# A decoder trunk on one Trainium2 core: turn-back sums of the state-space loop on TensorE, gate weights split after the loop, and another dealing-out of the table work

## The chip, the cores and the metric

The kernel runs on one core of one Trainium2 chip. The metric is the device time of one execution in microseconds. Times given as "the median" are over three timed runs; one further execution was taken by the hardware profiler, and all rows below are from that one.

## The reference, cut to what matters

Two layers of a trunk, on x of shape (1, 512, 1024) in float32. Each layer is FFN, token mixer, FFN, each between RMSNorms; the mixer of the first layer is the S5 state-space layer, that of the second a convolution module. The change touches the first FFN and the S5 layer:

```python
def swiglu(h, w1, w3, w2):
    return (jax.nn.silu(h @ w1) * (h @ w3)) @ w2

# s5_mixer: 64 groups, each with 64 complex states over 512 positions
u = (h @ w_in).reshape(bsz, seq, 64, 16)
... abar (decay and turn of each state), bb (its input weights) from dt, a, b
bu_re, bu_im = einsum(u, bb_re), einsum(u, bb_im)
_, _, st_re, st_im = lax.associative_scan(_complex_scan_op, elems, axis=1)
y = einsum(st_re, c_re) - einsum(st_im, c_im) + d_skip * u
y = gelu(y)
z = y * sigmoid(y @ w_glu + b_glu)
return z @ w_out
```

## The kernel before, in words

**Products.** Features lie on the 128 partitions, the 512 positions along the free axis. A weight unit is 128x1024 float32 (0.5 MB), that is eight 128x128 blocks. Each dense product is made of three fp32r products (`mm3`, lines 110 to 112): high weight part by high input part, high by low, low by high. `want(n)` makes the two parts of all units up to n: SP loads the raw unit (line 83, three raw buffers), ScalarE casts the high part (line 94), VectorE subtracts to get the low part (line 98). The load of unit u+3 is issued behind the split of unit u and waits for its raw buffer. Every engine works through its own queue in program order.

**First FFN.** 44 units of the up product (`ffn`), then 22 units of the down product (`proj`), 24 products each. Beside it the tables of the S5 layer are computed: generators, of which `tick(queue, budget)` runs some steps in every unit, until the estimated costs of the steps (in us) have used up the budget; what is overspent is taken off the next tick. The queue "D" (parameters, rotation tables) is served in the up product with the budget `PREP_UP`, the queue "P" in the down product with `PREP_DOWN`: first `s5_ops` for six tiles (costs 2.5 and 0.85 a tile), then `s5_in` for eight tiles (two steps of 2.1 a tile, lines 695 to 697 and 702 to 704, whose operands `bt` and `fb` come by the DMAs of lines 684 and 687). What is left of a queue is run by `flush` ahead of the last output block.

**S5 loop.** Eight tiles of 128x512, each four blocks of 128 (blocks of positions and features are regrouped through DRAM). The states are turned by a rotation, so that the recurrence is a real decay, scanned, and turned back. Step s issues `inputs(s)` (TensorE, line 867, 8 float32 products of 128 columns), `back(s-1)` (line 895 on), table loads for later tiles, and then, by the letters of `S5_ORDER[s]`: `stack` (k, line 855), `turn` (t, lines 880 to 885), `want` (w), `parts` (p, high and low part of y of tile s-3, lines 940 and 941), `state` (s, line 909), `decay` (d), `outputs(s-1)` (o, TensorE, lines 918 to 920, 12 float32 products), `scan` (c, line 892, two scans), `glu_step` (g, 12 fp32r products of the gate product) and `gelu` (l). The string `S5_ENG` says which engine does which sum or product:

```python
eng[0].tensor_tensor(X[:, 0], X[:, 0], Y[:, 0], op=A)        # turn, 882, POOL
eng[1].tensor_tensor(X[:, 1], X[:, 1], Y[:, 1], op=D)        # turn, 885, POOL
eng[2].tensor_tensor(S[:, 1, :, 1:], Y[:, 0, :, :n], s, op=M)  # back, 901, POOL
eng[3]... 902 DVE; eng[4]... 903 DVE; eng[5]... 904 POOL
eng[6].tensor_tensor(S[:, 1, :, 1:], S[:, 1, :, 1:], Y[:, 1, :, :n], op=A)  # 905, POOL
eng[7].tensor_tensor(st[i][:, 0, :, 1:], X[:, 0, :, :n], X[:, 1, :, :n], op=D)  # state, 909, DVE
```

`S5_WANT` says up to which unit step s splits: all eight gate units (u0+8 to u0+15) are split inside the loop. Only the first four of the eight output blocks of the gate product (`g4`) are accumulated in the loop; the other four (`h4`) come after it, and their products cover the trip of the last y through DRAM. Then follow `gates` for both halves and the output product.

Of the kernel before, what the change touches and what calls it, by code (L numbers as in the profile page):

```python
# [7 lines left out]
F32 = mybir.dt.float32  # L8
# [13 lines left out]

C_TAPS = (31, 31, None, None, None, None, None, 23)
NL = 2
S5_ORDER = ("sktwdopcgl", "sktwdopcgl", "stwdopcgkl", "skwtdopcgl", "skwtdopcgl", "skwtdolpcg", "skwtdopcgl", "skwtdopcgl", "skwtdopcgl")
S5_ENG = "PPPDDPPD"
S5_WANT = (8, 9, 10, 11, 11, 13, 14, 14, 15)
BUD_D = (3, 8, 18, 18, 18, 18)
FFN_AHEAD = 4

PREP_UP, PREP_DOWN = 2.8, 3.4
S5_FIRST = 2


# [1 line left out]
def trunk(ctx: ExitStack, tc: tile.TileContext, h, plan):  # L36
# [15 lines left out]
    def page(dt=F32R):  # L52
        return pages.tile([P, 2, T], dt, tag="pg", name=nm("pg"))
# [352 lines left out]
    def ffn(e, post, pre, defer=True):  # L406
        u0, xn = e["u"], e["xn"]
        g = []

        def evac(m, pa, pb):  # L410
            a = tmp()
            DVE.tensor_tensor(a, pa, e["y"], op=ALU.mult)  # L412
            ACT.activation(a, a, AF.Silu)  # L413
            DVE.tensor_tensor(a, pb, a, op=ALU.mult)  # L414
            t = page()
            ACT.copy(t[:, 0, :], a)  # L416
            DVE.tensor_tensor(t[:, 1, :], a, t[:, 0, :].bitcast(F32), op=ALU.subtract)  # L417
            g.append(t)

        pend = None  # L420
        want(u0 + 6)
        for m in range(2, NF):
            pa, pb = psum(), psum()
            for j, ps in enumerate((pa, pb)):
                want(u0 + 2 * m + j)
                for k in range(NK):
                    mm3(ps, u0 + 2 * m + j, k, xn[k][:, 0, :], xn[k][:, 1, :], k == 0, k == NK - 1)
                    if m == 2 and j == 0 and k == 4:
                        entry_norm(e, True)
                    if k == 3:  # L430
                        tick("D", PREP_UP)
            if FFN_AHEAD and m > 2:
                want(u0 + 2 * m + FFN_AHEAD)
            if m == 2:
                ACT.preload_act_table(AF.Silu)
                evac(0, e["ps"][0], e["ps"][1])
                evac(1, e["ps"][2], e["ps"][3])
            else:
                evac(*pend)
            pend = m, pa, pb  # L440
            want(u0 + 2 * m + 2)
        evac(*pend)
        return proj(u0 + 2 * NF, NF, g, post, 1, pre, g[:NK], carried=e["acc"], defer=defer)
# [234 lines left out]
    def s5_in():  # L678

        M, A, S = ALU.mult, ALU.add, ALU.subtract  # L680

        def load(i):
            bt, fb = page(F32), page(F32)
            nc.sync.dma_start(out=flat(bt), in_=h["s5b"][i, :, :1024])
            for t in range(4):
                src = f_d[t * 64 + i * 8 : t * 64 + i * 8 + 8, :].rearrange("r c -> (r c)")
                nc.sync.dma_start(out=flat(fb)[32 * t : 32 * t + 32, :], in_=src.partition_broadcast(32))
            return bt, fb

        nxt = load(0)  # L690
        yield
        for i in range(8):
            bt, fb = nxt
            t = page(F32)
            DVE.tensor_tensor(t[:, 0, :], fb[:, 1, :], bt[:, 1, :], op=M)
            DVE.tensor_tensor(t[:, 1, :], fb[:, 1, :], bt[:, 0, :], op=M)
            DVE.tensor_tensor(fb[:, 1, :], fb[:, 0, :], bt[:, 1, :], op=M)
            cost[0] += 2.1
            if i < 7:
                nxt = load(i + 1)  # L700
            yield
            DVE.tensor_tensor(fb[:, 0, :], fb[:, 0, :], bt[:, 0, :], op=M)
            DVE.tensor_tensor(fb[:, 0, :], fb[:, 0, :], t[:, 0, :], op=S)
            DVE.tensor_tensor(fb[:, 1, :], fb[:, 1, :], t[:, 1, :], op=A)
            nc.sync.dma_start(out=tab_d[i, :, 0:1024], in_=flat(fb))
            cost[0] += 2.1
            yield
# [124 lines left out]
    def s5(e, post, pre):  # L832
        u0, xn = e["u"], e["xn"]
        M, A, D = ALU.mult, ALU.add, ALU.subtract
        tabs, wk, st, yf, yhl, ys = {}, {}, {}, {}, {}, {}
        eng = [POOL if c == "P" else DVE for c in S5_ENG]
        quad = lambda v: v.rearrange("p (q c) -> p q c", q=4)
        n = P - 1

# [36 lines left out]
        def turn(i):  # L876
            b0, b1 = wk[i]
            c, s = tabs[i][2][:, 0], tabs[i][2][:, 1]
            X, Y = (page(F32).rearrange("p r (q c) -> p r q c", q=4) for _ in range(2))
            DVE.tensor_tensor(X[:, 0], b0, c, op=M)  # L880
            DVE.tensor_tensor(Y[:, 0], b1, s, op=M)
            eng[0].tensor_tensor(X[:, 0], X[:, 0], Y[:, 0], op=A)
            DVE.tensor_tensor(X[:, 1], b1, c, op=M)
            DVE.tensor_tensor(Y[:, 1], b0, s, op=M)
            eng[1].tensor_tensor(X[:, 1], X[:, 1], Y[:, 1], op=D)
            wk[i] = X, Y

        def scan(i):
# [5 lines left out]
                )  # L894

        def back(i):
            X, Y = wk[i]
            c, s = (tabs[i][2][:, r, :, :n] for r in range(2))
            S = st[i] = page(F32).rearrange("p r (q c) -> p r q c", q=4)
            POOL.memset(S[:, :, :, 0:1], 0.0)  # L900
            eng[2].tensor_tensor(S[:, 1, :, 1:], Y[:, 0, :, :n], s, op=M)
            eng[3].tensor_tensor(X[:, 1, :, :n], Y[:, 1, :, :n], s, op=M)  # L902
            eng[4].tensor_tensor(Y[:, 1, :, :n], Y[:, 1, :, :n], c, op=M)  # L903
            eng[5].tensor_tensor(X[:, 0, :, :n], Y[:, 0, :, :n], c, op=M)
            eng[6].tensor_tensor(S[:, 1, :, 1:], S[:, 1, :, 1:], Y[:, 1, :, :n], op=A)

        def state(i):
            X, Y = wk.pop(i)
            eng[7].tensor_tensor(st[i][:, 0, :, 1:], X[:, 0, :, :n], X[:, 1, :, :n], op=D)

        def outputs(i):
            q, mu = tabs[i][1], tabs[i][3]
            del tabs[i]
            S = st.pop(i)
            ps = psum()
            for j in range(4):
                o = ps[:, j * P : j * P + P]
                PE.matmul(o, lhsT=mu[:, 0, j, :], rhs=mu[:, 1, j, :], start=True, stop=False)
                PE.matmul(o, lhsT=q[:, 0, j, :], rhs=S[:, 0, j, :], start=False, stop=False)
                PE.matmul(o, lhsT=q[:, 1, j, :], rhs=S[:, 1, j, :], start=False, stop=True)  # L920
            return ps

        def gelu(i, ps):
# [13 lines left out]
        def parts(i):  # L937
            if i >= 0:
                t = yhl[i] = page()
                ACT.copy(t[:, 0, :], yf[i])  # L940
                DVE.tensor_tensor(t[:, 1, :], yf[i], t[:, 0, :].bitcast(F32), op=D)
# [14 lines left out]
        def glu_step(j0, bank, k):  # L956
            if k >= 0:
                for j in range(4):
                    mm3(bank[j], g0 + j0 + j, k, yhl[k][:, 0, :], yhl[k][:, 1, :], k == 0, k == NK - 1)

        load(0, (0, 3, 2))
        load(1, (0, 3, 2))
# [14 lines left out]
        for s in range(9):  # L977
            if s <= 7:
                inputs(s)
            if s <= 1:  # L980
                win(6 + s)
            if s == 3:
                g4.extend(psum() for _ in range(4))
            if s:
                back(s - 1)

            y_out(s - 2)
            load(s + 2, (0,))
            unstack(s + 2)
            load(s + 2, (2,))  # L990
            load(s + 1, (1,))
            y_in(s - 2)
            load(s + 3, (3,))
            wu = u0 + S5_WANT[s]
            for c in S5_ORDER[s]:
                if c == "t" and s <= 7:
                    turn(s)
                if c == "p":
                    parts(s - 3)
                if c == "s" and s:  # L1000
                    state(s - 1)
                if c == "k":
                    stack(s + 3)
                if c == "w":
                    want(wu)
                if c == "d":
                    decay(s + 1)
                if c == "c" and s <= 7:
                    scan(s)
                if c == "g":  # L1010
                    glu_step(0, g4, s - 3)
                if c == "o" and s:
                    po = outputs(s - 1)
                if c == "l" and s:
                    gelu(s - 1, po)
# [14 lines left out]

        y_out(7)
        parts(6)
        want(g0 + 7)
        y_in(7)
        h4.extend(psum() for _ in range(4))
        for k in range(3):
            glu_step(4, h4, k)
        glu_step(0, g4, 6)
        parts(7)
        glu_step(0, g4, 7)  # L1040
        ACT.preload_act_table(AF.Sigmoid)
        gates(g4, 0)
        for k in range(3, 8):
            glu_step(4, h4, k)
        want(g0 + 11)
        gates(h4, 4)
        return proj(
# [436 lines left out]
```

## Time and profile before

| | us |
|---|---|
| median of 3 runs | 1935.65 (1930.0 to 1937.69) |
| profiled execution | 1930.56 |
| its span, first to last instruction | 1928.4 |
| TensorE busy | 1867.4 (97%) |
| VectorE busy | 1100.8 (57%) |
| ScalarE busy | 636.9 (33%) |
| GpSimd (POOL) busy | 89.2 (5%) |

TensorE's mean granted clock is 0.988 of full speed. The first FFN lies at about 0 to 400 us of the span, the S5 layer at about 420 to 620 us, its loop at 438 to 538 us. A busy share is an average over the whole span; stretches are read one by one.

### The profile page before, as it was taken

To read this page: it belongs to the slowest core of one execution; us is meant where nothing else is said; L and a number is where in the kernel's file an instruction comes from. 1 tells how busy PE (TensorE), PEld (TensorE's weight loads), DVE (VectorE), ACT (ScalarE), POOL (GpSimd) and SP (SyncE) were. 2 spreads that over 40 slices of the span, in tenths; PEclk is the share of its full clock that TensorE was granted. 3 is DMA by queue.
4 is the path that set the end of the run, shared out by engine and by line. 5 is a ranking of instruction groups with operands and counts; after the bars stand their busy time and mean duration, and the time that the engine had idled before them with its cause. 6 is when DMAs were issued, how large, how long until landed. Compare 5 with 4: busy or idle time off the path is not lost.

```text
span 1928.4 us, 23797 instructions
## 1 busy us (share of the span) xinstructions
PE 1867.4 (97%) x9374; PEld 1587.3 (82%) x9374; DVE 1100.8 (57%) x1886; ACT 636.9 (33%) x920; POOL 89.2 (5%) x79
## 2 busy tenths in 40 slices
PE   9999999897799999999999999999999999999997
PEld 7788888796678888888898888888898888888886
DVE  6887465688946743432285433334995785343324
ACT  4323454251233532322244222223422653222211
POOL 2000000006700000000000000000000000000000
PEclk9999999998899999999999999999999999999998
DMA  4345458738522332222224322223464124232231
GB/s 159 110 134 156 136 134 252 238 141 303 184 83 77 106 113 98 89 86 98 88 77 131 101 96 88 76 99 98 170 230 142 52 70 153 88 101 85 89 98 44
DMA packets 101279, 235.04 MB, mean 122 GB/s; under 512 B 26160, under 2 KB 44080, under 8 KB 101168
## 3 DMA queue, kind: packets, MB, share of 16 engines
q1 hardware_dynamic: 99872, 232.46, 37.0%
q8 instruction: 73, 1.20, 0.3%
q10 hardware_dynamic: 1296, 1.07, 0.2%
q14 instruction: 38, 0.31, 0.1%
HBM read 209.77 MB, written 23.72 MB: 121 GB/s over the span
## 4 chain that ended last, share of the span: by engine, by line
PE 86%; DVE 9%; DMA 2%; issue 1%; ACT 1%; SPq 1%; POOLq 0%; POOL 0%; DVEq 0%; ACTq 0%
PE ps L112 27%; PE ps L111 27%; PE ps L110 27%; PE ps L1199 2%; DMA pg<-f_d 1%; DVE pg L98 1%; DVE pg L892 1%; PE ps L1166 1%; DVE x L354 1%; DVE tmp L350 1%; PE ps L740 1%; DVE pg L902 1%; PE ps L117 0%; DVE pg L186 0%; DVE pg L903 0%
## 5 line engine op out<-in xcount | busy, mean ns | idle before, releaser
L110 PE MATMUL ps<-pg,pg 128*128 128x512 f32 (+1 forms) x2808 | 1036.8, 369 | 7.4 <-ACT pg L1333 4.7
L112 PE MATMUL ps<-pg,pg 128*128 128x512 f32 (+1 forms) x2808 | 1029.8, 367 | 9.9 <-DVE pg L98 9.8
L111 PE MATMUL ps<-pg,pg 128*128 128x512 f32 (+1 forms) x2808 | 1031.8, 367 | 4.8 <-DVE pg L186 3.3
L112 PEld LDWEIGHTS ps<-pg,pg 128*128 128x128 f32 x2808 | 531.5, 189 | 97.9 <-DVE pg L98 11.9
L111 PEld LDWEIGHTS ps<-pg,pg 128*128 128x128 f32 x2808 | 531.6, 189 | 96.6 <-DVE pg L186 7.9
L110 PEld LDWEIGHTS ps<-pg,pg 128*128 128x128 f32 x2808 | 532.3, 190 | 95.5 <-ACT pg L1333 5.1
L98 DVE TENSOR_TENSOR pg<-raw,pg 128x1024 fp32r<-128x1024 f32 x305 | 368.3, 1244 | 109.9 <-ACT pg L94 63.5
L94 ACT CAST pg<-raw 128x1024 fp32r<-128x1024 f32 x310 | 311.2, 1047 | 108.7 <-DMA raw<-w 43.5
L414 DVE TENSOR_TENSOR tmp<-ps,tmp 128x512 f32<-128x512 f32 x88 | 60.9, 692 | 248.3 <-PE ps L112 219.2
L276 DVE TENSOR_TENSOR acc<-acc,tmp 128x512 f32<-128x512 f32 (+1 forms) x54 | 33.0, 611 | 255.2 <-ACT tmp L271 255.1
L413 ACT ACTIVATE tmp<-tmp 128x512 f32<-128x512 f32 x88 | 55.6, 632 | 284.8 <-DVE tmp L412 284.8
L416 ACT CAST pg<-tmp 128x512 fp32r<-128x512 f32 x88 | 54.6, 621 | 252.1 <-DVE tmp L414 249.5
L271 ACT ACTIVATE tmp<-ps 128x512 f32<-128x512 f32 (+1 forms) x45 | 24.3, 540 | 293.4 <-PE ps L112 293.0
L417 DVE TENSOR_TENSOR pg<-tmp,pg 128x512 fp32r<-128x512 f32 x88 | 61.0, 693 | 61.8 <-ACT pg L416 61.8
L412 DVE TENSOR_TENSOR tmp<-ps,y 128x512 f32<-128x512 f32 x88 | 60.4, 686 | 27.4 <-PE ps L112 27.4
L173 ACT ACTIVATE pg<-x,gsc 128x256 fp32r<-128x256 f32 x80 | 40.8, 510 | 67.8 <-DVE x L354 67.8
L1113 DVE SCALAR_TENSOR_TENSOR pg<-pg,vec,pg 128x512 f32<-128x512 f32 x79 | 53.0, 745 | 0.0
L186 DVE SCALAR_TENSOR_TENSOR pg<-x,gsc,pg 128x256 fp32r<-128x256 f32 (+1 forms) x88 | 47.9, 546 | 2.9 <-ACT pg L214 2.2
L354 DVE SCALAR_TENSOR_TENSOR x<-tmp,gsc,x 128x256 f32<-128x256 f32 x96 | 45.7, 477 | 0.0
L1199 PEld LDWEIGHTS ps<-pg,pg 128*128 128x128 f32 x360 | 40.9, 192 | 0.7 <-issue 0.4
L1199 PE MATMUL ps<-pg,pg 128*128 128x128 f32 x360 | 41.1, 275 | 0.0
L350 DVE TENSOR_TENSOR tmp<-pg,y 128x256 f32<-128x256 f32 x96 | 39.6, 418 | 0.4
(157 smaller groups left out, 885.2 us busy)
## 6 DMA issues: line engine op xcount, KB each, us to landing
raw<-w SPq DMA_DIRECT2D x262, 512.0 KB, 4.0
pg<-tab_d SPq DMA_DIRECT2D x24, 512.0 KB, 6.0
pg<-toep SPq DMA_DIRECT2D x20, 512.0 KB, 5.9
tab_d<-pg SPq DMA_DIRECT2D x16, 512.0 KB, 4.1
raw<-cv_w_in SPq DMA_DIRECT2D x16, 512.0 KB, 4.5
pg<-s5b SPq DMA_DIRECT2D x8, 512.0 KB, 7.2
pg<-f_d SPq DMA_DIRECT2D x32, 128.0 KB, 6.7
raw<-s_w_in SPq DMA_DIRECT2D x8, 512.0 KB, 4.3
```

The lines of the kernel that those rows point to most:

```text
L94: ACT.copy(hv, r)
L98: lo_engine[0].tensor_tensor(lv, r, hv.bitcast(F32), op=ALU.subtract)
L110: PE.matmul(out, lhsT=hi[:, s, :], rhs=xh, start=start, stop=False)
L111: PE.matmul(out, lhsT=hi[:, s, :], rhs=xl, start=False, stop=False)
L112: PE.matmul(out, lhsT=lo[:, s, :], rhs=xh, start=False, stop=stop)
L350: DVE.tensor_tensor(t[:, cs], hs[k][:, cs], y[:, cs], op=ALU.mult)
L354: DVE.scalar_tensor_tensor(x[:, k, cs], t[:, cs], gsc[:, post + k : post + k + 1], x[:, k, cs], op0=ALU.mult, op1=ALU.add)
L412: DVE.tensor_tensor(a, pa, e["y"], op=ALU.mult)
L413: ACT.activation(a, a, AF.Silu)
L414: DVE.tensor_tensor(a, pb, a, op=ALU.mult)
L417: DVE.tensor_tensor(t[:, 1, :], a, t[:, 0, :].bitcast(F32), op=ALU.subtract)
L1199: PE.matmul(ps[:, q * P : q * P + P], lhsT=op[ND * q + d], rhs=z[:, q, 8 - d : 8 - d + P], start=d == 0, stop=d == ND - 1,)
```

## The change

In the S5 loop the four turn-back products are no longer summed on VectorE or GpSimd. They go to two pages, S and X, one entry for each operand of each sum (one product with its sign turned), and `outputs` feeds all four to TensorE, which accumulates 20 instead of 12 products a tile. `state` is gone. One of the four products stays on GpSimd, three are on VectorE; of the two sums of `turn` one moves from GpSimd to VectorE. One order of letters serves all steps. The last four gate units are split after the loop, two by two, and the products of `h4` run block by block. In the first FFN the first four ticks have budgets of their own (4.5, 2.0, 0.0, 1.0), the down product's budget falls from 3.4 to 2.7, and `s5_in` issues the next tile's loads ahead of its first three products.

```diff
-S5_ORDER = ("sktwdopcgl", "sktwdopcgl", "stwdopcgkl", "skwtdopcgl", "skwtdopcgl", "skwtdolpcg", "skwtdopcgl", "skwtdopcgl", "skwtdopcgl")
-S5_ENG = "PPPDDPPD"
-S5_WANT = (8, 9, 10, 11, 11, 13, 14, 14, 15)
+S5_ORDER = "ktwpdocgl"
+S5_WANT = (8, 9, 10, 11, 11, 11, 11, 11, 11)
-PREP_UP, PREP_DOWN = 2.8, 3.4
+PREP_UP, PREP_DOWN = 2.8, 2.7
+PREP_FIRST = (4.5, 2.0, 0.0, 1.0)
@@ ffn
-                        tick("D", PREP_UP)
+                        n = 2 * m - 4 + j
+                        tick("D", PREP_FIRST[n] if n < len(PREP_FIRST) else PREP_UP)
@@ s5_in
             bt, fb = nxt
+            if i < 7:
+                nxt = load(i + 1)
             t = page(F32)
...
-            if i < 7:
-                nxt = load(i + 1)
@@ turn
-            eng[0].tensor_tensor(X[:, 0], X[:, 0], Y[:, 0], op=A)
+            POOL.tensor_tensor(X[:, 0], X[:, 0], Y[:, 0], op=A)
...
-            eng[1].tensor_tensor(X[:, 1], X[:, 1], Y[:, 1], op=D)
+            DVE.tensor_tensor(X[:, 1], X[:, 1], Y[:, 1], op=D)
@@ back
-            X, Y = wk[i]
+            X, Y = wk.pop(i)
...
-            POOL.memset(S[:, :, :, 0:1], 0.0)
-            eng[2].tensor_tensor(S[:, 1, :, 1:], Y[:, 0, :, :n], s, op=M)
...
-        def state(i):
-            X, Y = wk.pop(i)
-            eng[7].tensor_tensor(st[i][:, 0, :, 1:], X[:, 0, :, :n], X[:, 1, :, :n], op=D)
+            S = page(F32).rearrange("p r (q c) -> p r q c", q=4)
+            st[i] = S, X
+            for v in (S, X):
+                POOL.memset(v[:, :, :, 0:1], 0.0)
+            POOL.tensor_tensor(S[:, 0, :, 1:], Y[:, 0, :, :n], c, op=M)
+            DVE.scalar_tensor_tensor(X[:, 0, :, 1:], Y[:, 1, :, :n], -1.0, s, op0=M, op1=M)
+            DVE.tensor_tensor(S[:, 1, :, 1:], Y[:, 0, :, :n], s, op=M)
+            DVE.tensor_tensor(X[:, 1, :, 1:], Y[:, 1, :, :n], c, op=M)
@@ outputs
-                PE.matmul(o, lhsT=q[:, 0, j, :], rhs=S[:, 0, j, :], start=False, stop=False)
-                PE.matmul(o, lhsT=q[:, 1, j, :], rhs=S[:, 1, j, :], start=False, stop=True)
+                for r in range(2):
+                    for v in S:
+                        PE.matmul(o, lhsT=q[:, r, j, :], rhs=v[:, r, j, :], start=False, stop=r == 1 and v is S[1])
@@ behind the loop
         y_out(7)
         parts(6)
+        want(g0 + 5)
+        y_in(7)
         want(g0 + 7)
-        y_in(7)
         h4.extend(psum() for _ in range(4))
-        for k in range(3):
-            glu_step(4, h4, k)
         glu_step(0, g4, 6)
+        for j in range(4):
+            for k in range(4 if j == 3 else 5):
+                glu_part(4, h4, j, k)
         parts(7)
         glu_step(0, g4, 7)
         ACT.preload_act_table(AF.Sigmoid)
         gates(g4, 0)
-        for k in range(3, 8):
-            glu_step(4, h4, k)
+        for j in range(4):
+            for k in range(4 if j == 3 else 5, NK):
+                glu_part(4, h4, j, k)
         want(g0 + 11)
         gates(h4, 4)
```

## Rows read from the trace of the kernel before

**Rows 1.** The page, part 1: busy time, share of the span, instructions

```profile
PE 1867.4 (97%) x9374; PEld 1587.3 (82%) x9374; DVE 1100.8 (57%) x1886; ACT 636.9 (33%) x920; POOL 89.2 (5%) x79
```

**Rows 2.** Stretch in the loop: PE, PEld, DVE, ACT, POOL busy (count), clock, DMA share

```profile
460.00:480.00 20.00, 12.43 (x66) 11.33 (x67) 19.93 (x22) 3.26 (x5) 15.04 (x12) 0.74 0.81 276
```

**Rows 3.** Timeline of DVE: first, third, fourth and last of eight `state` sums

```profile
450.87 0.67 DVE L909 TENSOR_TENSOR pg<-pg 128x508 f32<-128x508 f32 x1
473.17 0.67 DVE L909 TENSOR_TENSOR pg<-pg 128x508 f32<-128x508 f32 x1
485.69 0.67 DVE L909 TENSOR_TENSOR pg<-pg 128x508 f32<-128x508 f32 x1
533.07 0.68 DVE L909 TENSOR_TENSOR pg<-pg 128x508 f32<-128x508 f32 x1
```

**Rows 4.** Timeline of DVE and POOL, step 3: start, duration, engine, operation, [idle before]

```profile
474.37 1.68 DVE L98 TENSOR_TENSOR pg<-raw,pg 128x1024 fp32r<-128x1024 f32 x1
475.98 0.68 DVE L880 TENSOR_TENSOR pg<-ps,pg 128x512 f32<-128x512 f32 x1
477.33 1.28 POOL L882 TENSOR_TENSOR pg<-pg,pg 128x512 f32<-128x512 f32 x1 [2.36 <-DVE pg L881]
478.37 0.79 DVE L941 TENSOR_TENSOR pg<-pg,pg 128x512 fp32r<-128x512 f32 x1
478.56 1.75 POOL L885 TENSOR_TENSOR pg<-pg,pg 128x512 f32<-128x512 f32 x1
479.08 3.42 DVE L892 TENSOR_TENSOR_SCAN pg<-acc,pg 128x512 f32<-128x512 f32 x2
481.46 2.10 POOL L901 TENSOR_TENSOR pg<-pg,pg 128x508 f32<-128x508 f32 x1 [1.07 <-DVE pg L892]
482.53 1.57 DVE L902 TENSOR_TENSOR pg<-pg,pg 128x508 f32<-128x508 f32 x1
484.14 1.63 DVE L903 TENSOR_TENSOR pg<-pg,pg 128x508 f32<-128x508 f32 x1
```

**Rows 5.** Timeline: first pair of scans, and `outputs(0)` from its first product to the next `inputs`

```profile
445.31 2.33 DVE L892 TENSOR_TENSOR_SCAN pg<-acc,pg 128x512 f32<-128x512 f32 x2
452.43 0.38 PE L918 MATMUL ps<-pg 128*128 128x128 f32 x2
455.11 1.95 PE L867 MATMUL ps<-pg,pg 128*128 128x128 f32 x16
```

**Rows 6.** Timeline of ACT behind the gate product: first sigmoid of each half, one cast

```profile
553.43 1.37 ACT L1023 ACTIVATE tmp<-ps,vec 128x512 f32<-128x512 f32 x2 [6.91 <-issue]
564.50 1.05 ACT L94 CAST pg<-raw 128x1024 fp32r<-128x1024 f32 x1 [2.96 <-DMA raw<-s_w_out]
567.03 1.38 ACT L1023 ACTIVATE tmp<-ps,vec 128x512 f32<-128x512 f32 x2 [1.48 <-PE ps L112]
```

**Rows 7.** Start of the first FFN: timelines of DVE, ACT and PE, and a stretch

```profile
37.09 0.69 DVE L125 SCALAR_TENSOR_TENSOR tmp<-tmp 128x512 f32<-128x512 f32 x1 [3.29 <-ACT tmp L123]
48.96 2.93 ACT L94 CAST pg<-raw 128x1024 fp32r<-128x1024 f32 x3
52.87 1.22 DVE L98 TENSOR_TENSOR pg<-raw,pg 128x1024 fp32r<-128x1024 f32 x1
54.14 0.50 PE L112 MATMUL ps<-pg,pg 128*128 128x512 f32 x1 [3.35 <-DVE pg L98]
50.00:100.00 50.00, 46.59 (x197) 38.12 (x198) 43.05 (x195) 15.66 (x20) 0.00 (x0) 0.97 0.32 106
```

**Rows 8.** Down product of the first FFN: PE timeline, a stretch, and a row of waits

```profile
345.83 0.50 PE L112 MATMUL ps<-pg,pg 128*128 128x512 f32 x1 [2.08 <-DVE pg L98]
365.72 0.80 PE L112 MATMUL ps<-pg,pg 128*128 128x512 f32 x1 [3.27 <-DVE pg L98]
365.00:370.00 5.00, 4.28 (x12) 3.44 (x13) 4.85 (x7) 0.25 (x1) 0.00 (x0) 0.66 0.44 153
DVE pg L695 <- DMA pg<-f_d: 22.1, 4, 11.8
```

More of the change, by code (lines that the diff above doesn't have):

```diff
@@ L835, in s5 @@
         tabs, wk, st, yf, yhl, ys = {}, {}, {}, {}, {}, {}
-        eng = [POOL if c == "P" else DVE for c in S5_ENG]
         quad = lambda v: v.rearrange("p (q c) -> p q c", q=4)
@@ L896, in back @@
         def back(i):
-            X, Y = wk[i]
+            X, Y = wk.pop(i)
             c, s = (tabs[i][2][:, r, :, :n] for r in range(2))
-            S = st[i] = page(F32).rearrange("p r (q c) -> p r q c", q=4)
-            POOL.memset(S[:, :, :, 0:1], 0.0)
-            eng[2].tensor_tensor(S[:, 1, :, 1:], Y[:, 0, :, :n], s, op=M)
[L902 to L905, printed above, removed]
-        def state(i):
-            X, Y = wk.pop(i)
-            eng[7].tensor_tensor(st[i][:, 0, :, 1:], X[:, 0, :, :n], X[:, 1, :, :n], op=D)
+            S = page(F32).rearrange("p r (q c) -> p r q c", q=4)
[6 more added lines that the diff above has]
+            DVE.tensor_tensor(X[:, 1, :, 1:], Y[:, 1, :, :n], c, op=M)
         def outputs(i):
@@ L958, in glu_step, with glu_part @@
                 for j in range(4):
-                    mm3(bank[j], g0 + j0 + j, k, yhl[k][:, 0, :], yhl[k][:, 1, :], k == 0, k == NK - 1)
+                    glu_part(j0, bank, j, k)
+        def glu_part(j0, bank, j, k):
+            mm3(bank[j], g0 + j0 + j, k, yhl[k][:, 0, :], yhl[k][:, 1, :], k == 0, k == NK - 1)
         load(0, (0, 3, 2))
@@ L994, in s5 @@
             wu = u0 + S5_WANT[s]
-            for c in S5_ORDER[s]:
+            for c in S5_ORDER:
                 if c == "t" and s <= 7:
@@ L999, in s5 @@
                     parts(s - 3)
-                if c == "s" and s:
-                    state(s - 1)
                 if c == "k":
```

## The prediction

> **What bounds the kernel now.** I read the page's busy shares first: TensorE is busy for 97% of the span [rows 1], so nearly everything is already paced by its products, and a change to other engines can win only what TensorE loses somewhere. Then I listed TensorE's idle times in order of time. They lie in three places that the change touches; each has its own limit, which the shares over the whole span hide.
>
> In the state-space loop TensorE worked for 12.43 of 20 us at a mean granted clock of 0.74, while VectorE was busy for 19.93 [rows 2]. So VectorE sets the step there. The eight `state` sums show the pace: from the first to the last 533.07 - 450.87 = 82.2 us for seven steps, 11.74 each [rows 3]. Inside one step [rows 4] the reader should see what makes VectorE slow. Products that read PSUM take 0.68 us, though GpSimd runs L882 beside them. Operations with both inputs in SBUF do not: L902 and L903 have as many elements and last 1.57 and 1.63, each beside a GpSimd operation (L901 ends at 483.56, L902 at 484.10); the two scans take 3.42 where GpSimd's L885 is in the way, and 2.33 where nothing is [rows 4, 5]. So either engine waits until the other has finished its operation, and GpSimd's four unlucky operations a step cost VectorE about 1 us each.
>
> At the start of the first FFN TensorE waits 3.35 us for the low part of a weight unit [rows 7]; in its down product it waits twice for the same reason, 2.08 and 3.27 us [rows 8], where VectorE itself had waited 22.1 us for the loads of `s5_in`. There one queue, VectorE's, holds table steps in front of weight splits.
>
> **The change part by part.** All times are laid against the profiled execution, 1930.6 us (span 1928.4 and 2.2 around it); the median is 5.1 above it.
>
> *The loop's step.* Step 3 of before, by the starts of VectorE's operations [rows 3, 4]: `state` and `stack` 1.20, split 1.61, four products of `turn` 2.39, `parts` 0.71, scans 3.45, L902 1.61, L903 1.55: together 12.52, which is the distance of the two sums. Afterwards: `stack` 0.60, four products 2.39; then the sum that moved from GpSimd, 0.60, behind GpSimd's own sum, which ends at 477.33 + 1.28, that is 0.24 after VectorE has come to it; `parts` 0.71; scans 2.36, since L885 is gone; three turn-back products at 0.60 and one block by GpSimd's remaining product, 1.0 (L902's 1.57 against a free 0.6). GpSimd's new memset of X has to follow the scan that reads X, and VectorE's first product may wait for it: 0 to 0.3, for which no row exists; between these ends nothing chooses, and I take 0.15. Sum 0.60 + 2.39 + 0.84 + 0.71 + 2.36 + 2.95 = 9.85. An undisturbed split adds 1.22 [rows 7]. Steps 1 and 2 have a split and no `parts`: 10.36 each; step 3 11.07; step 4 9.85; steps 5 to 7 have neither split nor `stack`: 9.25 each. Seven steps: 69.4 against 82.2, **12.8 us less**. Three splits (units 12 to 14, 1.22 to 1.61 each) that leave the loop are some 4 of that, the rest the sums and GpSimd's blocks. Bounds: if each GpSimd operation left (one sum, one product, two memsets) blocks once fully, about 1 us a step more, 6 us gained; if its product falls beside PSUM reads, 4 us more gained.
>
> *What TensorE pays.* `outputs` of before: 12 products in 455.11 - 452.43 = 2.68 us, 0.223 each [rows 5]. Eight more are 1.8 us a tile, 14.3 us over the loop. A gate product takes 0.227: 60 of them lie between the first sigmoids of the two halves, 13.60 us [rows 6]. A step then holds 8 + 20 float32 products and 12 gate products: 1.8 + 4.5 + 2.7 = 9.0 us. That is below the shortest VectorE step, 9.25, so the additions are hidden by VectorE's work, but only by 0.25; if VectorE were shorter, TensorE would be next at 9.0. Only the last tile shows its 1.8, of which the wait for the sum L905 gives 0.6 back: 1.2 lost. Loop: 12.8 - 1.2 = 11.6.
>
> *The splits behind the loop.* Units 12 to 15 are now split behind `parts(6)`: on ScalarE's queue four casts (1.05) and on VectorE's four subtractions (1.22) stand ahead of `parts(7)`; on SP's queue the load of the last y waits behind the loads of units 15 and 16, which wait for the low parts of 12 and 13. Cover: 24 gate products of g4's last two steps and 57 of h4, 81 x 0.227 = 18 us, against four casts and one subtraction (5.4 us) and then two DMAs of 0.26 MB: cost 0. Without that cover it would be up to 4 x (1.05 + 1.22) = 9 us. The price is at the other end: only 39 instead of 60 products lie between g4 and the output product. The cast of the fourth output weight unit ends 12.1 us behind g4's first sigmoid [rows 6], its low part 1.2 later, 13.3. TensorE now gets to it 9 + 39 + 11 products behind that sigmoid, 13.4. I charge 0.5 (0 to 2.4).
>
> *Order of letters, `decay`, queues.* With one order `stack`, `turn`, split, `parts` come before the scans in every step. Table loads move with the steps; in 460 to 480 us DMA was at 0.81 with 276 GB/s [rows 2], and they are issued two steps ahead, so I charge nothing; a fully busy DMA would cost a fraction of a step.
>
> *First ticks.* Costs noted in the code are 1.08, 1.44, 0.54, 1.26, 1.44, 0.54, 2.52 for the first steps. Before, ticks 0 to 2 ran three, two and two of them. With budgets 4.5, 2.0, 0 the first tick runs five, the second two, the third and fourth none. The two that moved up (15 operations, 2.7 by the notes, about 3 us) fall into VectorE's idle 3.29 us before the norm [rows 7]: just hidden; if they took longer, everything behind would slip by the excess. Nothing then stands before the third unit's low part: it starts when its cast ends, 48.96 + 1.05 = 50.0, instead of 52.87. TensorE's wait falls by 2.9. Behind it the clock was below full (0.97 over 50 us, 1.5 us) [rows 7], as behind the wait of 3.27 us (0.66 over 5 us) [rows 8]; with 0.45 us of waiting left I expect no slow clock. So 2.9 + 1.5 = **4.4 us** (2.9 to 4.9).
>
> *Down product.* A unit is 24 products, 5.4 us. At 3.4 a tick, an `s5_in` tile of 4.2 takes 1.24 units, 6.7 us; at 2.7 it takes 8.5. A tile moves three times 0.52 MB and its share of weights, 2.2 MB in 6.7 us or 2.4 in 8.5: 330 or 280 GB/s, against 276 / 0.81 = 340 for a full DMA [rows 2]. So before, the loads could hardly keep up, and each late load held up a split behind it; afterwards there is room of a sixth. The waits (5.35 us) and the slow clock after the second (0.34 x 5 = 1.7) are 7.0; I take **6** (0 to 7). By the notes one step (2.1) is left for `flush`; two units split ahead (10.9 us) hide it. Issuing the loads ahead of three products: SP does not wait for these, so 0; a page might come free later, 1 either way.
>
> Sum: 11.6 - 0.5 + 4.4 + 6 = 21.5. That gives 1909.1 on the profiled execution and 1914.2 on the median; I predict 1912.
>
> The Trainium skill, "SBUF — State Buffer", section "Who interferes with whom", says that a VectorE instruction with two SBUF inputs and a GpSimd instruction that reads SBUF exclude each other, and that the one that starts first blocks the other for its whole length. The rows agree (1.57 against 0.68). It speaks against part of this change: GpSimd keeps one such product beside three of VectorE.
>
> **The rivals.**
> - *GpSimd's product goes last.* VectorE's three products start first and GpSimd's comes behind; VectorE loses nothing, `outputs` starts 1 us later, and TensorE's 9.0 becomes the step. For it: no operation before had that constellation. Against: L885 and L901 each got their turn after one VectorE operation [rows 4]. 4 us better: 1908. By the rule of the Trainium skill named above it takes only that VectorE is first each time.
> - *GpSimd blocks several times a step*, as bounded above: 6 to 7 us lost, 1919.
> - *Loads of `s5_in` stay late*, because a tile's loads wait for pages or DMA is full anyway: the 6 us stay, 1918. With the one before: 1925, no change that can be told.
> - *Slower: TensorE's clock.* With 9.0 us of products in a 9.25 us step, the granted clock decides. At a mean c a step is 9.0/c; at 0.68 it is 13.2, and seven steps lose the 10 us won elsewhere. At 0.60 they are 23 us longer than now: 1948. For it: 0.74 in the loop now [rows 2]. Against: that clock stood where TensorE idled for 7.6 of 20 us, and idle time is what goes.
>
> **How the numbers follow.** Forecast 0.55, late loads 0.14, more blocks 0.10, both 0.09, GpSimd last 0.07, slow clock 0.05. The range leaves out the clock rival and little else: 1902 (all bounds good) to 1926. About 0.5%, 9.7 us, is what a measurement can tell: faster 0.85, same 0.10, slower 0.05.
>
> **What would show it.** Right: between the start of the second and the eighth `back` some 69 us instead of 82, scan pairs at 2.4, GpSimd at less than half its 89 us, TensorE's longest waits below 3 us; no slow clock at 55 us; no wait over 1 us between 320 and 370. Wrong: scan pairs or turn-back products still over 1.5, TensorE waiting for splits of units 12 to 15, steps set by TensorE at a clock below 0.9, or a new wait in front of the norm at 37 us.

## The result

The changed kernel takes 1902.3 us (median of four runs, 1900.6 to 1903.2) against 1932.8 (1928.5 to 1937.7) for the kernel before, measured beside it: a ratio of 0.984, 95% interval 0.981 to 0.987. That is 30.6 us less. The forecast was 1912, a gain of 21.5 on the profiled execution, with a range that began at 1902: the sign and the places were right, the size was about 30% too small, and the result lies at the very edge of the range. The profiled execution took 1902.2 us, span 1900.3.

Busy shares answer to [rows 1]. TensorE works as long as before, in a span that is 28 us shorter, with 64 products more; these count as 128 instructions, since a float32 product stands twice in the lists (the 8 of L867 are x16). GpSimd is at half. The page, part 1, of the changed kernel:

```profile
PE 1867.7 (98%) x9502; PEld 1590.8 (84%) x9502; DVE 1087.1 (57%) x1894; ACT 637.1 (34%) x920; POOL 44.2 (2%) x63
```

Stretches of the loop and of the two places in the first FFN, which answer to [rows 2], [rows 7] and [rows 8]; columns as in [rows 2]:

```profile
50.00:100.00 50.00, 48.66 (x214) 39.67 (x213) 40.12 (x161) 17.13 (x21) 0.00 (x0) 1.00 0.33 108
...
300.00:385.00 85.00, 84.67 (x432) 72.41 (x431) 58.04 (x86) 28.62 (x42) 0.00 (x0) 1.00 0.85 265
...
440.00:460.00 20.00, 16.55 (x130) 15.42 (x129) 19.86 (x25) 4.71 (x7) 6.19 (x10) 1.00 0.95 322
460.00:480.00 20.00, 19.75 (x135) 18.44 (x136) 19.86 (x26) 3.67 (x6) 6.18 (x10) 0.92 1.00 337
480.00:500.00 20.00, 20.00 (x156) 19.04 (x156) 19.86 (x27) 2.94 (x5) 6.94 (x11) 1.00 0.44 145
```

The reader should see three things. Behind the start of the FFN the clock is full, where it was 0.97 of it. Over the down product TensorE is idle for 0.33 of 85 us. In the loop, TensorE now works for all of 480 to 500 us, while VectorE is as busy as before: neither has slack there.

One step of the loop, VectorE and GpSimd of the changed kernel, which answers to [rows 4] (the scan is L892, the three turn-back products on VectorE are L906 to L908, the one on GpSimd L905, the sum that moved is L885); ahead of it and behind it the loop's first and last turn-back:

```profile
436.57 0.69 DVE L906 SCALAR_TENSOR_TENSOR pg<-pg,pg 128x508 f32<-128x508 f32 x1
...
474.70 2.33 DVE L892 TENSOR_TENSOR_SCAN pg<-acc,pg 128x512 f32<-128x512 f32 x2
477.07 0.69 DVE L906 SCALAR_TENSOR_TENSOR pg<-pg,pg 128x508 f32<-128x508 f32 x1
477.21 1.67 POOL L905 TENSOR_TENSOR pg<-pg,pg 128x508 f32<-128x508 f32 x1
477.68 1.75 DVE L907 TENSOR_TENSOR pg<-pg,pg 128x508 f32<-128x508 f32 x1
479.35 0.68 DVE L908 TENSOR_TENSOR pg<-pg,pg 128x508 f32<-128x508 f32 x1
479.95 0.68 DVE L880 TENSOR_TENSOR pg<-ps,pg 128x512 f32<-128x512 f32 x1
...
481.31 1.27 POOL L882 TENSOR_TENSOR pg<-pg,pg 128x512 f32<-128x512 f32 x1 [2.42 <-DVE pg L881]
481.75 0.68 DVE L884 TENSOR_TENSOR pg<-ps,pg 128x512 f32<-128x512 f32 x1
482.46 0.69 DVE L885 TENSOR_TENSOR pg<-pg,pg 128x512 f32<-128x512 f32 x1
483.07 0.68 DVE L941 TENSOR_TENSOR pg<-pg,pg 128x512 fp32r<-128x512 f32 x1
483.67 2.33 DVE L892 TENSOR_TENSOR_SCAN pg<-acc,pg 128x512 f32<-128x512 f32 x2
...
503.96 0.69 DVE L906 SCALAR_TENSOR_TENSOR pg<-pg,pg 128x508 f32<-128x508 f32 x1
```

From scan to scan 8.97 us, with every operation at its free duration but L907, which GpSimd's product holds up for 1.07 us. The scans take 2.33, not 3.42. From the first turn-back (436.57) to the last (503.96) seven steps take 67.4 us; before, they took 82.2 [rows 3].

TensorE in the same loop: the first product of `inputs` of the later steps (L867), and the two longest waits:

```profile
458.69 1.90 PE L920 MATMUL ps<-pg,pg 128*128 128x128 f32 x8 [3.10 <-POOL pg L905]
...
467.91 1.95 PE L867 MATMUL ps<-pg,pg 128*128 128x128 f32 x16
...
477.49 1.95 PE L867 MATMUL ps<-pg,pg 128*128 128x128 f32 x16
...
486.53 1.95 PE L867 MATMUL ps<-pg,pg 128*128 128x128 f32 x16
...
495.52 1.95 PE L867 MATMUL ps<-pg,pg 128*128 128x128 f32 x16
...
505.81 1.63 PE L920 MATMUL ps<-pg,pg 128*128 128x128 f32 x8 [0.93 <-POOL pg L905]
```

Set side by side product by product, the two profiled executions give: start of the FFN 4.5 us less, down product 7.9 less, loop 17.6 less, tail behind the gate product 0.5 more, and 1.7 more in the first 52 us; this is there by 17 us, ahead of everything the change touches. The sum, -27.8, is the difference of the spans (28.1) within 0.3.

### The profile page after: what moved, and what is told of

The parts are those of the page before. It is cut to its first block, busy times and chain, and to the rows that moved or that the text cites. A ratio compares the mean times of both kernels' runs of the same rounds, so it can differ in the third digit from the quotient of the medians.

```text
span 1900.3 us, 24034 instructions
## 1 busy us (share of the span) xinstructions
PE 1867.7 (98%) x9502; PEld 1590.8 (84%) x9502; DVE 1087.1 (57%) x1894; ACT 637.1 (34%) x920; POOL 44.2 (2%) x63
## 3 DMA queue, kind: packets, MB, share of 16 engines
q10 hardware_dynamic: 1296, 1.07, 0.2%
## 4 chain that ended last, share of the span: by engine, by line
PE 85%; DVE 8%; DMA 4%; issue 1%; ACT 1%; SPq 1%; DVEq 0%; ACTq 0%
PE ps L112 27%; PE ps L111 27%; PE ps L110 27%; PE ps L1203 2%; DMA pg<-f_d 1%; DVE pg L98 1%; DMA pg<-s5b 1%; DVE pg L892 1%; DVE pg L907 1%; PE ps L1170 1%; DVE x L354 1%; DVE tmp L350 1%; PE ps L741 1%; DVE pg L186 1%; PE ps L117 1%
## 5 line engine op out<-in xcount | busy, mean ns | idle before, releaser
L98 DVE TENSOR_TENSOR pg<-raw,pg 128x1024 fp32r<-128x1024 f32 x305 | 362.1, 1224 | 111.0 <-ACT pg L94 75.7
L173 ACT ACTIVATE pg<-x,gsc 128x256 fp32r<-128x256 f32 x80 | 40.8, 510 | 67.4 <-DVE x L354 67.4
L186 DVE SCALAR_TENSOR_TENSOR pg<-x,gsc,pg 128x256 fp32r<-128x256 f32 (+1 forms) x88 | 48.4, 551 | 3.4 <-ACT pg L214 2.9
L1203 PE MATMUL ps<-pg,pg 128*128 128x128 f32 x360 | 41.0, 275 | 0.0
L920 PE MATMUL ps<-pg,pg 128*128 128x128 f32 x256 | 36.6, 285 | 4.5 <-POOL pg L905 4.0
```

The lines of the kernel that those rows point to most:

```text
L98: lo_engine[0].tensor_tensor(lv, r, hv.bitcast(F32), op=ALU.subtract)
L186: DVE.scalar_tensor_tensor(xn[k][:, 1, cs], x[:, k, cs], g, xn[k][:, 0, cs].bitcast(F32), op0=ALU.mult, op1=ALU.subtract)
L1203: PE.matmul(ps[:, q * P : q * P + P], lhsT=op[ND * q + d], rhs=z[:, q, 8 - d : 8 - d + P], start=d == 0, stop=d == ND - 1,)
```

## The experiments

Each kernel was timed beside the kernel before, whose median was 1932.9 to 1933.2 there.

**First ticks alone.** The kernel before, with the budgets of the first four ticks:

```diff
+PREP_FIRST = (4.5, 2.0, 0.0, 1.0)
...
-                        tick("D", PREP_UP)
+                        n = 2 * m - 4 + j
+                        tick("D", PREP_FIRST[n] if n < len(PREP_FIRST) else PREP_UP)
```

> The kernel before with the four first-tick budgets alone. Theory (the places are independent and their gains add): TensorE's wait of 3.35 us at 54 us falls to about 0.5 and the slow clock behind it goes, 4.4 us less in all, 1928 to 1929 beside a median of 1933; nothing else moves. Rival (five steps do not fit into the idle time before the norm): a new wait near 37 us and 0 to 2 us less.

Measured: 1929.0, ratio 0.9981 (0.9971 to 0.9990), 4.1 us less. TensorE's waits at the start (lines are one further down in this kernel):

```profile
51.12 0.51 PE L111 MATMUL ps<-pg,pg 128*128 128x512 f32 x1 [0.80 <-ACT pg L95]
52.38 0.50 PE L113 MATMUL ps<-pg,pg 128*128 128x512 f32 x1 [0.53 <-DVE pg L99]
```

The wait of 3.35 [rows 7] is 0.53, and the granted clock of 50 to 60 us is 1.00, where it was 0.83 in the kernel before. The term stands as predicted (4.4).

**Budget of the down product alone.**

```diff
-PREP_UP, PREP_DOWN = 2.8, 3.4
+PREP_UP, PREP_DOWN = 2.8, 2.7
```

> The kernel before with 2.7 instead of 3.4 for the down product alone; the loads stay where they were. Theory (the loads were asked for faster than they come): the waits of TensorE between 320 and 370 us go, 6 to 8 us less. Rival (the order of loads and pages did it): the waits stay, 0 to 2 us less.

Measured: 1923.9, ratio 0.9950 (0.9935 to 0.9965), 9.2 us less, more than the 6 to 8 expected. TensorE does not wait at all between 300 and 385 us. But the loads are not earlier for it. VectorE's waits for them (total, times, longest):

```profile
DVE pg L695 <- DMA pg<-f_d: 23.8, 4, 12.8
```

VectorE waits 23.8 us for `f_d`, no less than the 22.1 before [rows 8] (24.5 in the changed kernel), and the first products of the eight tiles lie 58.3 us apart from first to last (320.88 to 379.20) against 55.9 before (309.81 to 365.75). So a tile takes some 8 us under either budget, and VectorE waits for loads under either. (At 2.7 the budget alone asks for 8.5 us a tile; the pace does not tell budget from loads there, the waits do.) What changed is what stands between such a wait and the next weight split: before, the product that waited 4.10 us (359.26) was followed by five more of `s5_in` ahead of the low part at 364.45, for which TensorE then waited; with 2.7 the one that waited 5.78 us (371.79) is followed by two (low part at 375.00), and TensorE does not wait. That fewer table steps in front of a split are the cause is read from the order of VectorE's operations and was not tried by itself.

**Order of the loads in `s5_in` alone.**

```diff
             bt, fb = nxt
+            if i < 7:
+                nxt = load(i + 1)
             t = page(F32)
...
-            if i < 7:
-                nxt = load(i + 1)
             yield
```

> The kernel before with the loads of s5_in issued ahead of the first three products, budget 3.4 as before. Theory: 0, at most 1 us either way. Rival: the order of pages did it, 6 to 8 us less.

Measured: 1933.1, ratio 0.9995 (0.9983 to 1.0008): nothing, as expected. The waits of the down product stay:

```profile
346.99 0.67 PE L112 MATMUL ps<-pg,pg 128*128 128x512 f32 x1 [2.13 <-DVE pg L98]
...
367.15 0.50 PE L112 MATMUL ps<-pg,pg 128*128 128x512 f32 x1 [1.95 <-DVE pg L98]
```

**Late gate splits alone.** `S5_WANT` and the order behind the loop as in the change, the sums as before:

```diff
-S5_WANT = (8, 9, 10, 11, 11, 13, 14, 14, 15)
+S5_WANT = (8, 9, 10, 11, 11, 11, 11, 11, 11)
...
         parts(6)
+        want(g0 + 5)
+        y_in(7)
         want(g0 + 7)
-        y_in(7)
...
```

> The kernel before with the last four gate units split behind the loop and the products of h4 block by block; sums stay on VectorE and GpSimd. Theory: steps 5 and 6 of the loop fall from 13.65 and 12.52 us to the 10.3 of a step without split, 5.5 us less, and 0.5 comes back behind the gate product: 5 us less. Rival (the splits come back as a stall of TensorE behind the loop): waits for units 12 to 15 of 5 us or more, 0 us less.

Measured: 1930.8, ratio 0.9985 (0.9972 to 0.9998), 2.3 us less, half of what was expected. From one L902 to the next, step 6 fell from 12.54 to 10.33 us (step 7, without a split in either kernel, stays at 10.3), but step 5 only from 13.67 to 12.77. VectorE and ScalarE there:

```profile
495.41 3.42 DVE L892 TENSOR_TENSOR_SCAN pg<-acc,pg 128x512 f32<-128x512 f32 x2
...
507.53 0.60 ACT L925 ACTIVATE tmp<-ps 128x512 f32<-128x512 f32 x1 [7.99 <-PE ps L920]
508.02 0.61 ACT L940 CAST pg<-pg 128x512 fp32r<-128x512 f32 x1
508.66 0.69 DVE L941 TENSOR_TENSOR pg<-pg,pg 128x512 fp32r<-128x512 f32 x1 [3.58 <-ACT pg L940]
...
509.27 2.33 DVE L892 TENSOR_TENSOR_SCAN pg<-acc,pg 128x512 f32<-128x512 f32 x2
```

In the order of letters of the kernel before, `gelu` stands ahead of `parts` in step 5 ("skwtdolpcg"). So the cast L940 waits on ScalarE behind the gelu (L925), which waits for the products of `outputs`, and VectorE waits 3.58 us for that cast. Before, two splits filled this time.

**Late splits with step 5 in the order of its neighbours.** That reading was tried by one edit more, in the sixth entry of `S5_ORDER`:

```diff
-"skwtdolpcg"
+"skwtdopcgl"
```

> The late splits alone, as before, and step 5's order of letters set to that of its neighbours, so that the gelu stands behind parts. Theory: with the old order the cast of parts on ScalarE stood behind the gelu and so behind the products of the step before, VectorE waited for it, and step 5 fell to 12.80 us only; with the order of the other steps it falls to about 10.3 like steps 6 and 7, seven steps take 76.6 us instead of 79.1, and the gain against the kernel before is 4 to 5 us instead of 2.3 (about 1928.5 beside 1933). Rival: the wait in step 5 has another source (the sums or GpSimd's operations of the step before), the order does nothing, step 5 stays near 12.8 and the gain near 2.3 us.

The steps did as the theory said. The last four pairs of scans:

```profile
495.52 3.40 DVE L892 TENSOR_TENSOR_SCAN pg<-acc,pg 128x512 f32<-128x512 f32 x2
...
505.84 3.42 DVE L892 TENSOR_TENSOR_SCAN pg<-acc,pg 128x512 f32<-128x512 f32 x2
...
516.15 3.40 DVE L892 TENSOR_TENSOR_SCAN pg<-acc,pg 128x512 f32<-128x512 f32 x2
...
526.46 3.42 DVE L892 TENSOR_TENSOR_SCAN pg<-acc,pg 128x512 f32<-128x512 f32 x2
```

All are 10.3 apart, and seven steps take 76.7 us (453.22 to 529.91 by L902) against 79.2 with the old order and 82.2 before. The time is 1929.9. The medians differ by 3.0 us; the ratio, 0.9976 (0.9964 to 0.9987), goes by the means, which differ by 4.7, with an interval of 2.5 to 7.0. The 4 to 5 expected lie in it, but the timing alone does not tell the two edits apart (0.4 to 5.4 with the old order). The traces do: product by product TensorE's loop is 5.5 us shorter than before, with the old order 2.2. In both, 0.5 us is paid back behind the loop, the tail's price. So late splits bring their whole gain only where the order of step 5 is changed with them.

**Sums on TensorE alone.** Four turn-back products on two pages and 20 products in `outputs`, as in the change; splits, orders and budgets as before:

```diff
-S5_ENG = "PPPDDPPD"
...
+            POOL.tensor_tensor(S[:, 0, :, 1:], Y[:, 0, :, :n], c, op=M)
+            DVE.scalar_tensor_tensor(X[:, 0, :, 1:], Y[:, 1, :, :n], -1.0, s, op0=M, op1=M)
+            DVE.tensor_tensor(S[:, 1, :, 1:], Y[:, 0, :, :n], s, op=M)
+            DVE.tensor_tensor(X[:, 1, :, 1:], Y[:, 1, :, :n], c, op=M)
...
```

> The kernel before with the new turn, back and outputs alone (TensorE adds up four products a tile); order of letters, budgets and splits as before. Theory (the loop's 17.6 us are 5.5 from the splits and the rest from the sums): 12 us less, steps without split near 9. Rival (TensorE's 64 added products show, 0.22 us each, or the splits carry most): under 6 us less.

Measured: 1918.4, ratio 0.9926 (0.9911 to 0.9941), 14.9 us less, where 12 were expected. The first and the last turn-back on VectorE (lines are one further up here):

```profile
454.46 0.69 DVE L905 SCALAR_TENSOR_TENSOR pg<-pg,pg 128x508 f32<-128x508 f32 x1
...
524.83 0.69 DVE L905 SCALAR_TENSOR_TENSOR pg<-pg,pg 128x508 f32<-128x508 f32 x1
```

Seven steps take 70.4 us, so of the 14.8 us that the steps gained in the change (82.2 to 67.4) the sums alone give 11.8; late splits and the single order give 3.0 more on top of them. The sums are half of the whole gain. The five parts add up: 4.1 + 9.2 + 0 + 2.3 + 14.9 = 30.5, against 30.6 for the change (31.2 with 3.0 for the late splits). That they agree to 0.1 is luck: each part has an interval of some 2 to 3 us to either side.

**Is it the sums, or GpSimd?** The kernel before with its five operations a step on GpSimd given to VectorE:

```diff
-S5_ENG = "PPPDDPPD"
+S5_ENG = "DDDDDDDD"
```

> The kernel before with all eight sums and products of turn, back and state on VectorE. Theory (an operation of GpSimd keeps VectorE waiting about as long as VectorE would need for it): step 4 is 18 operations of 0.6 or so and two scans, 10.8 instead of 10.9 us, the whole within 3 us of before. Rival (GpSimd takes work off VectorE): five more operations of 0.6 a step, 3 us a step, 20 to 24 us more.

Measured: 1930.9, ratio 0.9987 (0.9977 to 0.9996), 2.2 us *less* than before, with five operations more a tile on the engine that sets the step. Step 4 takes 10.99 us (10.8 expected, 10.88 before). VectorE in it:

```profile
499.50 2.33 DVE L892 TENSOR_TENSOR_SCAN pg<-acc,pg 128x512 f32<-128x512 f32 x2
501.75 0.66 DVE L901 TENSOR_TENSOR pg<-pg,pg 128x508 f32<-128x508 f32 x1
502.33 0.68 DVE L902 TENSOR_TENSOR pg<-pg,pg 128x508 f32<-128x508 f32 x1
503.04 0.69 DVE L903 TENSOR_TENSOR pg<-pg,pg 128x508 f32<-128x508 f32 x1
```

L902 and L903 last 0.68 and 0.69, where they took 1.57 and 1.63 beside GpSimd [rows 4], and the scans 2.33 for 3.42. These three had cost VectorE 2.9 us a step (0.89, 0.94 and 1.09), about what five operations of 0.6 cost it now: dealing the work out to GpSimd had saved VectorE nothing. So the sums' gain is that the additions are gone from both engines, not that GpSimd was relieved.

**The last product off GpSimd.** The changed kernel with all four turn-back products on VectorE:

```diff
-            POOL.tensor_tensor(S[:, 0, :, 1:], Y[:, 0, :, :n], c, op=M)
+            DVE.tensor_tensor(S[:, 0, :, 1:], Y[:, 0, :, :n], c, op=M)
```

> The changed kernel with the last product of back on VectorE too; GpSimd keeps the one sum of turn. Theory: GpSimd's block of 1.07 becomes 0.6, a step without split 8.5 on VectorE; TensorE's 9.0 a step is then the bound of steps 4 to 7, so 1 to 2 us less than the changed kernel. Rival 1 (TensorE has more room than that): 0.47 a step, 3.8 us less. Rival 2 (GpSimd runs beside): 4 to 5 us more.

Measured: 1896.1, ratio 0.9809 (0.9793 to 0.9825) to the kernel before: 6.2 us less than the changed kernel by the medians, and the fastest of all. The profiled executions differ by 5.6. Product by product, 1.5 us of it are the first 50 us, which were short in this run, 0.6 the end of the first FFN, which this edit does not touch, and 4.1 the loop; 0.7 goes the other way near the end. The product that stood behind GpSimd's lasts 0.68, where it took 1.75:

```profile
473.58 0.68 DVE L907 TENSOR_TENSOR pg<-pg,pg 128x508 f32<-128x508 f32 x1
```

TensorE's `inputs`, its waits, and a stretch (columns as in [rows 2]):

```profile
454.15 0.46 PE L920 MATMUL ps<-pg,pg 128*128 128x128 f32 x2 [1.50 <-POOL pg L904]
454.79 1.90 PE L920 MATMUL ps<-pg,pg 128*128 128x128 f32 x6 [0.18 <-DVE pg L906]
464.00 1.95 PE L867 MATMUL ps<-pg,pg 128*128 128x128 f32 x16
473.01 1.95 PE L867 MATMUL ps<-pg,pg 128*128 128x128 f32 x16
...
490.98 1.95 PE L867 MATMUL ps<-pg,pg 128*128 128x128 f32 x16
440.00:460.00 20.00, 18.26 (x144) 17.64 (x143) 19.93 (x28) 4.71 (x7) 3.09 (x11) 0.91 0.94 325
```

TensorE's steps are 9.00 us, without a wait from 464 us to the loop's end: its own work. VectorE's seven steps take 64.0 us instead of 67.4; each of the first five is 0.62 shorter, the sixth 0.35, the last none. The expectation was too low: it let TensorE's 9.0 bind from step 4 on (1 to 2 us less), but only the last two steps of VectorE show it. In size rival 1 (3.8) came out, though TensorE did bind in the end. The early wait of 3.10 us is 1.50 and 0.18 here.

**What TensorE pays.** The changed kernel with four more float32 products a tile (the first of each block is issued twice, and the second starts the sum anew, so nothing else changes):

```diff
+                PE.matmul(o, lhsT=mu[:, 0, j, :], rhs=mu[:, 1, j, :], start=True, stop=True)
                 PE.matmul(o, lhsT=mu[:, 0, j, :], rhs=mu[:, 1, j, :], start=True, stop=False)
```

> The changed kernel with four more float32 products a tile in outputs, the first of each block done twice: 0.9 us of TensorE a step, nothing for the others. Theory (9.0 us of products in a step of 8.96): steps 4 to 7 and the last tile show it all, 4 to 5 us more than the changed kernel. Rival 1 (TensorE has room): only the last tile, 1 us more. Rival 2 (TensorE is the bound in all steps): 7 us more.

Measured: 1903.8, ratio 0.9850 (0.9835 to 0.9865), 1.5 us more than the changed kernel by the medians, where 4 to 5 were expected. The steps of TensorE are 9.88 apart, 0.88 more than in the kernel above:

```profile
457.92 1.63 PE L921 MATMUL ps<-pg,pg 128*128 128x128 f32 x8 [1.95 <-POOL pg L905]
...
467.19 1.95 PE L867 MATMUL ps<-pg,pg 128*128 128x128 f32 x16
477.07 1.95 PE L867 MATMUL ps<-pg,pg 128*128 128x128 f32 x16
486.95 1.95 PE L867 MATMUL ps<-pg,pg 128*128 128x128 f32 x16
```

So 0.22 us a product is confirmed, and TensorE becomes the bound: VectorE's last two steps are 9.16 and 9.88, where they were 8.96. Yet eight tiles x 0.9 us are 7 us of work, and product by product the loop is only 2.2 us longer: the added products first fill the wait of the early steps (1.95 instead of 3.10), and the granted clock of 430 to 470 us is 1.00 where it was 0.96, which gives 1.7 us back. Without that the loop would be 3.9 us longer, near the theory. By the time alone rival 1, that TensorE has room (1 us), could not be told from it; the steps of 9.88 are what speaks against it.

## Why the prediction was right and wrong

Two terms of the sum failed. The loop (11.6 forecast, 17.6 found) was right in its mechanism and mis-sized, most of all in its last tile. The down product (6 forecast, 7.9 and 9.2 found) was wrong in its mechanism too: the loads did not arrive in time, as the prediction had it, but stayed as late as before.

**Right, as mechanisms.** VectorE set the loop's step, and GpSimd's operations held it up: the scans fell from 3.42 to 2.33, and giving GpSimd's work to VectorE cost nothing. (The price was three disturbed operations, 2.9 us a step, somewhat less than the four of about 1 us that the prediction counted.) The rule that the prediction took from the Trainium skill ("SBUF — State Buffer", section "Who interferes with whom") agrees with the kernels in which it was tried: L907 lasts 1.75 beside GpSimd's one product and 0.68 without it, and L902 and L903 last 0.68 and 0.69 where GpSimd does none of this work. That GpSimd's product blocks VectorE once a step at about 1.0 us (measured 1.07), rather than several times or never, was right too, so both rivals on GpSimd fall; taking that one product off GpSimd makes the loop of the fastest kernel 4.1 us shorter. The start of the FFN (4.4 forecast, 4.5 between the profiles, 4.1 timed), the norm just ahead of it (VectorE's idle 3.29 is filled, 0.57 left) and the tail (0.5 charged, 0.5 found) are as worked out. TensorE's wait in the tail is 0.23, not the 9 us that no cover would have cost:

```profile
543.49 0.50 PE L112 MATMUL ps<-pg,pg 128*128 128x512 f32 x1 [0.23 <-DVE pg L98]
```

**The loop: 11.6 forecast, 17.6 found.** The mechanism was right, and three terms of the sum were mis-sized.
- *The step.* 9.85 for step 4 and 9.25 for steps 5 to 7 were forecast; 9.56 and 8.97 came out. `parts` was 0.11 too long (0.71 was read in front of a scan that GpSimd held up; undisturbed it is 0.60), the wait ahead of the sum L885 0.13 (0.24 charged, 0.11 found), and the 0.15 for a wait behind the memset doesn't exist: L906 starts directly behind the scan; GpSimd's block is 0.07 longer than charged. Over seven steps that is 67.4 instead of 69.4, 2.0 us.
- *The last tile.* The prediction charged 1.2 us, as if the eight more products simply came on top. In fact `outputs(7)` starts behind GpSimd's product at 505.81, while VectorE is at its second and has the third to do, where it used to wait for L905 and `state`. From the start of the last turn-back to the end of these products it is 6.6 us instead of 8.3, and the gate products behind it no longer begin at a low clock, another 0.6. So 2.3 won in place of 1.2 lost, 3.5 us. Most of the 2.3 is the clock, which the prediction left out here: in the kernel before it was granted at 0.57 from 536 to 540 us, behind these waits, which costs 1.7 us; in the changed kernel it is full behind the wait of 0.93.
- *The first step*, ahead of the seven, gave 0.5 that was not counted.

Together 6.0, which is the difference. The stretch of the low clock in the kernel before (columns as in [rows 2]):

```profile
536.00:540.00 4.00, 4.00 (x18) 3.70 (x17) 0.84 (x2) 1.10 (x2) 0.00 (x0) 0.57 0.43 131
```

Not charging for DMA held: its share reached 1.00 in 460 to 480 us without a wait on VectorE's side.

**The down product: 6 forecast, 7.9 between the profiles, 9.2 timed.** The forecast size came from the waits of one execution. It left out the third wait there (0.76), and that execution was a mild one. Take the stretch from the FFN's first low part (the second of the waits at its start) to the S5 layer's first wait (L186), less what a low clock behind the first of them costs (1.7 or 3.4 us by the granted clock of 52 to 67 us, nothing where the first ticks were changed). With the budget of 3.4 it is 354.0 us in the kernel before, and 352.5, 355.1, 356.1, 356.5, 357.4 and 359.1 in the six experiments that keep that budget. With 2.7 it is 345.7, 345.6, 345.6 and, in the changed kernel, 346.2. So the stall costs 7 to 13 us in these seven traces, 10 on their mean, and 8 in the one on which the prediction stood. They are traces of seven kernels, and only one of the edits (the order of the loads, 352.5) lies in this stretch; that it is the execution that varies is supported by the times, if weakly: their standard deviation is 1.7 to 3.6 us in the experiments with this stall and 0.5 to 1.8 us in the four kernels without it. The sums alone show the worst of it:

```profile
337.59 0.79 PE L112 MATMUL ps<-pg,pg 128*128 128x512 f32 x1 [3.77 <-DVE pg L98]
...
372.40 0.79 PE L112 MATMUL ps<-pg,pg 128*128 128x512 f32 x1 [4.97 <-DVE pg L98]
```

The bounds, 0 to 7, came from the same single execution and were too narrow for the same reason. The mechanism failed as well: the prediction let the loads arrive in time because a tile would take 8.5 instead of 6.7 us. A tile took 8.0 already, and VectorE waits for the loads as long as before; why the stall went all the same is argued above, not shown. The rival that they stay late was right about the loads and wrong about the 6 us: it took for granted that late loads must delay the splits.

**The time.** The forecast took 1912, between 1909.1 from the profiled execution and 1914.2 from the median, and so treated the 5.1 us between the two as an offset that stays. Half of it was the small number of runs: with 13 and 25 runs the median of the kernel before is 1932.9 to 1933.2, 2.3 to 2.6 above the profiled execution. And part of what remains does not stay: the down product's stall is 2 us larger on the mean than in the profiled execution, and the change removes it whole. The first 50 us, below, were also short in that execution. Against the medians the gain is 30.6, between the profiles 28.4. Of the 9.1 us by which the sum of 21.5 falls short, 6.0 are the loop (by the profiles) and 3.2 the down product (as timed).

**The other rivals.** The slow-clock one did not come: the granted clock is 1.00 where TensorE has no gap and 0.92 in one stretch behind the wait of 3.10. But its first premise was nearly met: a step of 8.97 on VectorE and 9.0 on TensorE leaves no slack, and in the kernel with four more products the last step takes all of the 0.9 us added.

## What to carry to other kernels

Size a stall that is paced by loads from several executions, not from one: the profiled one can be the mild one, and the part of the median's offset that such a stall makes goes away with it. Work given to a second engine that excludes the first one saved nothing here; take it to an engine that idles (here TensorE, at 0.22 us a product), and look at the next bound (9.0 against 8.97 us a step) before giving it more. Edits that move work out of a step should be tried with the order of the step: in the traces the late splits alone won 2.2 us of the loop, with one letter moved 5.5.

## What the runs showed that was not expected

The first 50 us vary: TensorE's first product behind the wait of 0.8 us starts between 50.05 (the kernel before as profiled) and 53.70 us (all sums on VectorE). Most of the difference is there by 17 us, ahead of every edit. Single profiles therefore differ by up to 3.6 us before the stretch of interest begins, and were compared from a common product on. The length of a wait alone does not tell whether TensorE's clock falls behind it: the granted clock was 0.92 in the stretch behind a wait of 3.10 us and 1.00 throughout the stretch that holds a wait of 1.95, but 0.91 in the stretch of 440 to 460 us that holds a wait of only 1.50 and one of 0.18 (all turn-back products on VectorE), where the products behind these two waits ran at the lower level. Where it stood at the lower level, 1.2 GHz, float32 products followed each other at 0.43 us instead of 0.22 (the kernel before at 536 us, behind waits of 2.10 and 0.63).
